# A routed-expert kernel on one core: rows gathered from three bf16 parts, an embedding normed later, a test moved forward

## The chip, the cores and the metric

The kernel runs on one core of a Trainium2 chip. The metric is device time in microseconds of one launch, as the median of several runs. TensorE (PE; its weight loads are PEld) multiplies, VectorE (DVE), ScalarE (ACT) and GpSimd (POOL) work on elements, and SyncE (SP) mostly issues transfers. POOL and ACT issue transfers too. Each engine works through its own queue in order, and engines wait for each other through semaphores.

## What is computed

Two transformer blocks, one behind the other, on 512 tokens of width 1024. The first ends in a layer of 64 experts in 8 groups: a token goes to its best group and the two best experts in it.

```
g_idx = top_k(softmax(h @ w_group + b_group), 1)
top_v, top_i = top_k(e_logits of that group, 2)
gate = g_w * softmax(top_v)
y[e] = (silu(x_e @ w1[e]) * (x_e @ w3[e])) @ w2[e]      # w1, w3: 1024 x 512, w2: 512 x 1024, fp32
out[token] += gate * y
```

The second block has retention and latent attention, a feed-forward layer, and at its end an embedding per layer (PLE):

```
e = rmsnorm(p @ w_ple_proj, ple_norm)
h = h + e * sigmoid(h @ w_ple_gate + b_ple_gate)
```

## The kernel before

All 64 experts are worked through in 16 groups of four (`q`), each expert with at most 32 tokens (`CAP`). The weights of the experts stream from memory in loads of 1 MB, in the order of `moe_specs`: for each group w1, w3, w2, each in two halves of four experts. SP issues them in that order from `moe_load_to`, as far ahead as slots are free. Each half product of `moe_up` or `moe_back` asks for loads 13 places ahead (`AHEAD`), and such a load waits until the product that used its slot is through.

Ahead of the experts stands the end of the attention. In the loop over four tiles of 128 tokens the last projection is added (`x_add`, L844), the rows are normed (L924, `x1n(t)`, fp32), transposed and scaled (`turn_tok`, `h` at L895) and multiplied to logits (L908). Then VectorE works out the routing in a chain of small operations (L953 to L978) that ends in `osel`, the selected experts in bf16. Products with a triangle of ones (L984 to L988) count for each token its place in its expert, and `places_oh(q)` compares places with 0 to 31 (L998), which gives the one-hot matrix `oh` of a group.

`moe_gather(q)` takes the rows of a group's tokens by multiplying: `x1n` is the stationary operand, `oh` the moving one, both fp32 (L1016), in two halves of 512 columns of the model. VectorE evacuates each half with the norm's gain (L1017) into `xT`. In group 0 the first half is gathered, then comes the first half product (L1029), then the second half of the gather, then the second half product. For the later groups the two halves of the gather of group q+1 stand between the half products of group q.

The PLE embedding is made at the same time, in units (`ple_units`) that a generator puts between other work: products and copies to `er` (L802), sums of squares (L823, L824), then the norm itself: ACT's scale (L806) and POOL's multiplication (L807) for tile 0, one VectorE operation each for the others (L814). POOL stores the normed tiles to memory (L808, L815). At the end of the kernel `ple_gate` loads them back and uses them (L1784 to L1789).

An expert with more than 32 tokens is left to `moe_rest`. It reads the largest count into a register on each engine (L1090) and branches (L1091); in this run the branch isn't taken. `REST_AT` = 8 puts it behind group 8, and `moe_lim` stops the loads at that point. On the way past the branch SP waits for the semaphores of its transfers.

Of the kernel before, what the change touches and what calls it, by code (L numbers as in the profile page):

```python
# [26 lines left out]
REST_AT = 8  # L27
# [44 lines left out]
def tile_kernel(ctx: ExitStack, tc: tile.TileContext, a: dict, dbg=None, upto=9):  # L72
# [712 lines left out]
    def ple_proj(pin, wst):  # L785
        pT = HL("pT", 2, 512, 2, M)
# [7 lines left out]
        lnb = bcast("lnb", a["ple_norm_2"])  # L794
        yield
        for t in range(NT):
            for nh in range(2):
# [7 lines left out]
                if t == 1 and nh == 1:  # L805
                    ACT.activation(ER[0], ER[0], AF.Copy, scale=ERS[0])  # L806
                    POOL.tensor_mul(ER[0], ER[0], lnb)  # L807
                    POOL.dma_start(e_d[0], ER[0])  # L808
# [4 lines left out]
        for t in (1, 2, 3):  # L813
            DVE.scalar_tensor_tensor(ER[t], ER[t], ERS[t], lnb, op0=ALU.mult, op1=ALU.mult)  # L814
            POOL.dma_start(e_d[t], ER[t])  # L815
            yield

    ERS = {}

    def ple_sums(t):  # L820

        rs = ERS[t] = sm("rs_e", (128, 1))
        POOL.tensor_scalar(rs, sum_sq(ER[t], D), 4.0 / D, 4.0 * EPS, op0=ALU.mult, op1=ALU.add)  # L823
        POOL.tensor_tensor(rs, rs, mhalf, op=ALU.pow)  # L824
# [29 lines left out]
    moe_w, moe_also, moe_n, moe_lim = {}, {}, [0], [24 * REST_AT + 37]  # L854

    def moe_load_to(n):
        n = min(n, moe_lim[0])
# [39 lines left out]

    h2 = {}
# [17 lines left out]
    for t in range(NT):  # L916
# [62 lines left out]
    ple_units(7)  # L979
# [15 lines left out]
    def places_oh(q):  # L995
        oh = Sx("oh", (128, NT, 4, 32))
# [11 lines left out]
    def moe_gather(q, hfs=range(2)):  # L1008
# [78 lines left out]
    def moe_rest():  # L1087
# [3 lines left out]
        with tc.If(most > CAP):  # L1091
            gov = Sx("gov", (128, NT, 64))
            DVE.scalar_tensor_tensor(gov, rk, CAP - NOT_SEL - 0.5, gate, op0=ALU.is_ge, op1=ALU.mult)
            hT_, hid, w2_, wk = L("hTo", (128, 8, 256)), M("hido", (128, 4, 256)), M("w2o"), [M("wko"), M("wko")]
            w2q = w2_.rearrange("p (j n) -> p j n", j=4)
            ps, s_, g1 = [PS() for _ in range(4)], Sx("so"), sm("g1", (128, NT))
            for ts in HALVES:
                for u, t in enumerate(ts):
                    for hf in range(2):
                        p = ps[2 * u + hf].rearrange("p (c s) -> p c s", c=4)  # L1100
                        for c in range(4):
                            PE.transpose(p[:, c], x1c(t)[:, 4 * hf + c], ident)
                        DVE.tensor_tensor(hT_[:, 4 * hf:4 * hf + 4, 128 * u:128 * u + 128], p,
                                          gr[:, 4 * hf:4 * hf + 4, None].to_broadcast([128, 4, 128]), op=ALU.mult)
# [733 lines left out]
```

## Time and profile before

| | us |
| --- | --- |
| median of 3 runs | 2050.45 |
| lowest and highest run | 2049.34, 2050.8 |
| profiled run | 2050.91 |
| span of the profiled run | 2048.8 |
| busy: PE, PEld | 1905.1, 1274.1 |
| busy: DVE, ACT, POOL | 744.6, 468.4, 208.8 |
| moved | 510.18 MB, 249 GB/s on the mean |

The page gives the busy time of each engine, then the span in 40 equal slices of 51.2 us with what the transfers moved in each. The share of an engine is a mean over stages with different limits: the attention ahead (up to about 337 us), the experts (to about 1320 us) and the second block behind. A timeline gives start, duration, engine, line, operation and names; in square brackets stands the idle time of the engine before it, and what ended that.

### The profile page before, as it was taken

To read this page: it belongs to the slowest core of one execution; us is meant where nothing else is said; L and a number is where in the kernel's file an instruction comes from. 1 tells how busy PE (TensorE), PEld (TensorE's weight loads), DVE (VectorE), ACT (ScalarE), POOL (GpSimd) and SP (SyncE) were. 2 spreads that over 40 slices of the span, in tenths; PEclk is the share of its full clock that TensorE was granted. 3 is DMA by queue.
4 is the path that set the end of the run, shared out by engine and by line. 5 is a ranking of instruction groups with operands and counts; after the bars stand their busy time and mean duration, and the time that the engine had idled before them with its cause. 6 is when DMAs were issued, how large, how long until landed. Compare 5 with 4: busy or idle time off the path is not lost.

```text
span 2048.8 us, 24118 instructions
## 1 busy us (share of the span) xinstructions
PE 1905.1 (93%) x9932; PEld 1274.1 (62%) x9932; DVE 744.6 (36%) x1392; ACT 468.4 (23%) x841; POOL 208.8 (10%) x159
## 2 busy tenths in 40 slices
PE   8999999998899888889988889799999999999998
PEld 6877778864344444434443434268877888888877
DVE  4364565421111111111112211157474642444465
ACT  5454433200000000000000100053235433323232
POOL 1010002200000000000000000044034310101031
PEclk9999999999999999999999999899999999999999
DMA  8122125799999999998999999973113214141342
GB/s 280 37 78 70 45 103 212 285 397 422 421 421 420 421 421 421 421 421 370 421 421 420 421 421 421 395 246 100 27 52 117 90 42 144 52 134 57 114 133 67
DMA packets 148725, 510.18 MB, mean 249 GB/s; under 512 B 20033, under 2 KB 77178, under 8 KB 100610
## 3 DMA queue, kind: packets, MB, share of 16 engines
q1 hardware_dynamic: 144226, 501.92, 62.8%
q0 software_dynamic: 1824, 6.31, 0.8%
q8 instruction: 80, 1.31, 0.3%
q10 hardware_dynamic: 2560, 0.35, 0.1%
q14 instruction: 35, 0.29, 0.0%
HBM read 502.24 MB, written 6.31 MB: 248 GB/s over the span
## 4 chain that ended last, share of the span: by engine, by line
PE 25%; DMA 18%; issue 5%; DVE 4%; ACT 1%; POOL 1%; SPq 0%; ACTq 0%; POOLq 0%; DVEq 0%
DMA w<-in_w_dram 18%; PE g L282 2%; PE g L284 2%; PE g L283 2%; PE u L282 1%; PE u L284 1%; PE u L283 1%; PE d L282 1%; PE d L284 1%; PE d L283 1%; PE pg L283 1%; PE pg L284 1%; PE pg L282 1%; PE ps L1029 1%; DVE h L1639 1%
## 5 line engine op out<-in xcount | busy, mean ns | idle before, releaser
L1029 PE MATMUL ps<-w,xT 128*32 128x512 f32 x2040 | 301.2, 627 | 60.2 <-DMA w<-in_w_dram 55.3
L1016 PEld LDWEIGHTS g<-oh,x1n 128*128 128x128 f32 x1024 | 246.2, 334 | 26.9 <-issue 19.3
L1016 PE MATMUL g<-oh,x1n 128*128 128x128 f32 x1024 | 252.3, 405 | 0.8 <-DVE oh L998 0.8
L1017 DVE TENSOR_TENSOR xT<-g,gr 128x512 f32<-128x512 f32 x32 | 22.1, 692 | 578.0 <-PE g L1016 578.0
L1029 PEld LDWEIGHTS ps<-w,xT 128*32 128x32 f32 x2040 | 71.4, 114 | 255.5 <-issue 128.6
L1043 PE MATMUL y<-w,hT 128*32 128x512 f32 x960 | 171.5, 686 | 48.3 <-DMA w<-in_w_dram 43.6
L1043 PEld LDWEIGHTS y<-w,hT 128*32 128x32 f32 x960 | 39.5, 122 | 166.6 <-DMA w<-in_w_dram 84.9
L1077 DVE TENSOR_TENSOR acc<-acc,spread 128x512 f32<-128x512 f32 x128 | 87.8, 688 | 122.7 <-PE spread L1072 122.7
L1072 PE MATMUL spread<-y,gt 128*128 128x512 f32 x256 | 118.4, 605 | 1.5 <-ACT y L1060 0.8
L226 POOL TENSOR_TENSOR c0l<-c0r,c0h 128x1024 fp32r<-128x1024 f32 x2 | 4.7, 2360 | 937.4 <-DMA c1r<-in_w_in_dram 937.4
L1280 ACT ACTIVATE hT<-hT 128x512 f32<-128x512 f32 x16 | 9.6, 597 | 360.8 <-PE hT L1278 360.8
L1072 PEld LDWEIGHTS spread<-y,gt 128*128 128x128 f32 x256 | 46.0, 189 | 73.3 <-issue 63.1
L1269 ACT ACTIVATE sl<-ps 128x512 f32<-128x512 f32 x16 | 9.6, 597 | 278.3 <-PE ps L1029 278.3
L1047 ACT COPY y<-y 128x512 f32<-128x512 f32 x30 | 17.6, 586 | 200.8 <-PE y L1043 194.9
L1704 POOL TENSOR_TENSOR aTl<-sg,aTh 128x512 fp32r<-128x512 f32 x18 | 23.4, 1297 | 225.9 <-ACT aTh L1703 178.5
L1702 DVE TENSOR_TENSOR sg<-sg,u 128x512 f32<-128x512 f32 x22 | 15.1, 688 | 72.0 <-PE u L284 70.9
L1703 ACT CAST aTh<-sg 128x512 fp32r<-128x512 f32 x22 | 13.7, 621 | 105.0 <-DVE sg L1702 105.0
L1271 DVE TENSOR_TENSOR hd<-sl,ps 128x512 f32<-128x512 f32 x16 | 11.0, 688 | 51.2 <-PE ps L1029 51.2
L174 POOL TENSOR_TENSOR rs<-ms,mhalf 128x1 f32<-128x1 f32 x20 | 12.0, 601 | 169.1 <-DVE ms L172 169.1
L1700 ACT ACTIVATE sg<-zg 128x512 f32<-128x512 f32 x22 | 13.9, 632 | 62.5 <-DVE zg L1699 62.5
L604 ACT ACTIVATE sc<-sc,mn 128x128 f32<-128x128 f32 (+3 forms) x32 | 17.7, 555 | 44.7 <-DVE mn L600 44.7
L768 POOL TENSOR_TENSOR mTl<-gl,mTh 128x512 fp32r<-128x512 f32 x8 | 11.5, 1454 | 157.7 <-PE ps L284 145.8
(1206 smaller groups left out, 3912.1 us busy)
## 6 DMA issues: line engine op xcount, KB each, us to landing
w<-in_w_dram SPq DMA_DIRECT2D x375, 1024.0 KB, 19.8
w<-in_w_dram SPq DMA_DIRECT2D x16, 512.0 KB, 13.9
x<-in_x_dram SPq DMA_DIRECT2D x4, 512.0 KB, 3.7
cb<-cum_d POOLq DMA_DIRECT2D x8, 256.0 KB, 3.6
acc<-in_x_dram SPq DMA_DIRECT2D x4, 512.0 KB, 7.5
e_d<-er POOLq DMA_DIRECT2D x4, 512.0 KB, 3.9
h_d<-u POOLq DMA_DIRECT2D x4, 512.0 KB, 6.6
h<-h_d SPq DMA_DIRECT2D x4, 512.0 KB
```

Of the source, the lines that this page charges most:

```text
L282: PE.matmul(out, ah, bh, start=(start and c == 0), stop=False)
L283: PE.matmul(out, ah, bl, start=False, stop=False)
L284: PE.matmul(out, al, bh, start=False, stop=(stop and c == kt - 1))
L604: ACT.activation(sc, sc, AF.Exp, bias=mn[:, s:s + 1], scale=-1.0, accum_out=su[:, s:s + 1])
L1016: PE.matmul(p[:, c], x1c(t)[:, 4 * hf + c], OHG[q][0][:, t].rearrange("p e s -> p (e s)"), start=(t == 0), stop=(t == NT - 1))
L1017: DVE.tensor_tensor(xT[:, 4 * hf:4 * hf + 4], p, gr[:, 4 * hf:4 * hf + 4, None].to_broadcast([128, 4, 128]), op=ALU.mult)
L1029: PE.matmul(p[32 * e:32 * e + 32], XT[q][:, 4 * hf + c, 32 * e:32 * e + 32], w[c] if isinstance(w, list) else w[:, c], start=(hf + c == 0) ...
L1043: PE.matmul(ps[nh][32 * e:32 * e + 32], HT[q][:, j, 32 * e:32 * e + 32], moe_w[2, q, hf, e][:, j - 2 * hf, 512 * nh:512 * nh + 512], start ...
L1072: PE.matmul(p, gt[:, t], Y[q][:, 512 * nh:512 * nh + 512], start=True, stop=True)
L1077: DVE.tensor_add(av(t)[:, sl], av(t)[:, sl], p)
L1639: DVE.tensor_add(av(t), av(t), v)
L1704: (eng or POOL).tensor_sub(aT.lo(c), s_, aT.hi(c).bitcast(F32))
```

## The change

- **Planes.** A new function `x_planes(t, eng)` splits each tile of `x1n` into three bf16 parts that add up to it: ACT casts the tile to `hi`, the engine `eng` subtracts it in place, ACT casts the rest to `mid`, the engine subtracts once more into `lo`. For tiles 0 and 1 the engine is VectorE, for 2 and 3 POOL. It is called in the loop over the tiles behind `logits_a(t - 1)`, for the last tile behind `logits_a(3)`.
- **Gather.** `oh` is bf16, and each fp32 product of the gather becomes three bf16 products into the same sum.
- **Group 0.** The whole gather stands ahead of the first product; the units of the embedding are all done before.
- **Test.** The largest count and its cast stand right behind the gather of group 0, and `moe_rest` behind the arithmetic of the gates, ahead of the first product. `REST_AT` and `moe_lim` go. The branch's body, not executed here, is rewritten for one tile at a time.
- **Embedding.** POOL stores the tiles without the norm, at the start of `ple_sums`. The scale is kept in `ers`, and `e_gain`, one VectorE operation for each of eight halves, applies scale and gain at the end. The gain `lnb`, 512 KB when it is spread over the partitions, is loaded at the end too.
- **Slots.** `pT` takes one slot of the weights' pool instead of two of the middle one.

```diff
+    def x_planes(t, eng):
+        hm = M("xb", (128, 2, 8, 128), BF)
+        if t % 2 == 0:
+            XL[t // 2] = M("xbl", (128, 2, 8, 128), BF)
+        v, XP[t] = x1c(t), (hm[:, 0], hm[:, 1], XL[t // 2][:, t % 2])
+        ACT.copy(XP[t][0], v)
+        eng.tensor_sub(v, v, XP[t][0])
+        ACT.copy(XP[t][1], v)
+        eng.tensor_sub(XP[t][2], v, XP[t][1])
...
             logits_a(t - 1)
+            x_planes(t - 1, POOL if t == 3 else DVE)
...
     logits_a(3)
+    x_planes(3, POOL)
...
-    ple_units(7)
+    ple_units(9)
...
-        oh = Sx("oh", (128, NT, 4, 32))
+        oh = Sx("oh", (128, NT, 4, 32), BF)
...
-                    PE.matmul(p[:, c], x1c(t)[:, 4 * hf + c], OHG[q][0][:, t].rearrange("p e s -> p (e s)"), start=(t == 0), stop=(t == NT - 1))
+                    for k in range(3):
+                        PE.matmul(p[:, c], XP[t][k][:, 4 * hf + c], OHG[q][0][:, t].rearrange("p e s -> p (e s)"),
+                                  start=(t == 0 and k == 0), stop=(t == NT - 1 and k == 2))
...
     places_oh(0)
-    ple_units(3)
-    moe_gather(0, (0,))
-    ple_units(1)
+    moe_gather(0)
     moe_load_to(15)
-    p1 = moe_up(0, 1, 0, lambda: moe_gather(0, (1,)))
...
+    cmax = const.tile([128, 1], F32, name="cmax")
+    DVE.tensor_reduce(cmax, pc[:, :64], axis=AX.X, op=ALU.max)
+    cmax_i = const.tile([128, 1], I32, name="cmax_i")
+    DVE.tensor_copy(cmax_i, cmax)
...
     DVE.tensor_tensor(gate, fl(oa), fl(ob), op=ALU.add)
+    moe_rest()
+    p1 = moe_up(0, 1, 0)
...
-        if q == REST_AT:
-            moe_rest()
-            moe_lim[0] = len(moe_specs)
...
-    bpl = bcast("bpl", a["b_ple_gate_2"])
+    bpl, lnb = bcast("bpl", a["b_ple_gate_2"]), bcast("lnb", a["ple_norm_2"])
...
+    def e_gain(k):
+        t, nh = divmod(k, 2)
+        DVE.scalar_tensor_tensor(es[k], es[k], ers[:, t:t + 1], lnb[:, 512 * nh:512 * nh + 512],
+                                 op0=ALU.mult, op1=ALU.mult)
...
+            if t == NT - 1 and nh == 1:
+                e_gain(2 * t + nh)
...
+            if n == 512:
+                e_gain(2 * t + nh)
```

What stands in a row on SP before, at the test behind group 8 (`w` are loads of weights, `cmax_i` is the largest count), and the way out of the branch:

```order
L880 DMA w_1104_5621<-in_w_dram 128x2048 [waits DMAHW7_49,PE_49]
L880 DMA w_1105_5623<-in_w_dram 128x2048 [waits DMAHW0_49,PE_49]
L1090 TENSOR_LOAD cmax_i [waits DVE_49]
L1090 ISA x2
...
L1091 UNCONDITIONAL_BRANCH [waits DMAHW0_49,DMAHW1_49,DMAHW2_49,DMAHW3_49,DMAHW4_49,DMAHW5_49,DMAHW6_49,DMAHW7_49]
```

There loads stand directly ahead of the test, and the branch waits for the semaphores of all eight. The same on SP after, in group 0 (`w13s` are the four pieces of the fifteenth weight):

```order
L867 DMA w13s_3550<-in_w_dram 128x512 [waits DMAHW3_49,DMASW4_49,Activation_49]
L867 DMA w13s_3551<-in_w_dram 128x512 [waits DMASW7_49,DMAHW4_49,DMASW0_49,DVE_49]
L867 DMA w13s_3552<-in_w_dram 128x512 [waits DMAHW5_49,Activation_49]
L1097 TENSOR_LOAD cmax_i [waits DVE_49]
L1097 ISA x2
L1098 COMPARE_AND_BRANCH
...
L1098 UNCONDITIONAL_BRANCH [waits DMAHW0_49,DMAHW1_49,DMAHW2_49,DMAHW3_49,DMAHW4_49,DMAHW5_49,DMAHW6_49,DMAHW7_49]
L870 DMA w_700_4213<-in_w_dram 128x2048 [waits DMAHW6_49,PE_49]
```

The test has moved behind the fifteen loads that fit the slots, and the sixteenth stands behind the branch. On VectorE before, in the loop over the tiles (`acc` are the rows, `wo` the projection's sum, `h` the scaled transposes, `lg` the logits):

```order
L895 TENSOR_TENSOR h_611_3153<-tt_3154,gr 128x512
L895 TENSOR_TENSOR h_611_3153<-tt_3160,gr 128x512
L908 TENSOR_TENSOR lg_2867<-lg_3166,rb 128x72
L844 TENSOR_TENSOR acc_2670<-acc_2670,wo_615_3176 128x512
L172 TENSOR_SCALAR ms_3204<-ss_3202 128x1
L924 TENSOR_SCALAR x1n_3208<-acc_2670,rs_3206 128x1024
```

and after, at the same place:

```order
L885 TENSOR_TENSOR h_611_3157<-tt_3158,gr 128x512
L885 TENSOR_TENSOR h_611_3157<-tt_3164,gr 128x512
L897 TENSOR_TENSOR x1n_3102<-x1n_3102,xb_3170 128x8x128
L899 TENSOR_TENSOR xbl_3118<-x1n_3102,xb_3170 128x1024
L911 TENSOR_TENSOR lg_2868<-lg_3175,rb 128x72
L835 TENSOR_TENSOR acc_2670<-acc_2670,wo_616_3185 128x512
L171 TENSOR_SCALAR ms_3213<-ss_3211 128x1
L927 TENSOR_SCALAR x1n_3217<-acc_2670,rs_3215 128x1024
```

The two subtractions of tile 1's planes now stand ahead of the addition of the projection of tile 3; those of tile 0 stand in the same way ahead of tile 2's.

## Rows read from the trace of the kernel before

**Rows 1.** The page's slices of the span: GB/s that the transfers moved in each.

```profile
GB/s 280 37 78 70 45 103 212 285 397 422 421 421 420 421 421 421 421 421 370 421 421 420 421 421 421 395 246 100 27 52 117 90 42 144 52 134 57 114 133 67
```

**Rows 2.** The page's groups (busy us, mean ns) and its transfers (count, KB, us to landing).

```profile
L1016 PE MATMUL g<-oh,x1n 128*128 128x128 f32 x1024 | 252.3, 405 | 0.8 <-DVE oh L998 0.8
...
w<-in_w_dram SPq DMA_DIRECT2D x375, 1024.0 KB, 19.8
```

**Rows 3.** Windows: length, busy PE, PEld, DVE, ACT, POOL, granted clock, DMA share, GB/s.

```profile
388.00:398.00 10.00, 8.45 (x40) 8.04 (x44) 5.60 (x9) 2.12 (x4) 5.61 (x9) 0.83 0.77 285
...
412.00:416.00 4.00, 4.00 (x44) 1.17 (x36) 3.13 (x15) 0.60 (x1) 0.00 (x0) 1.00 0.57 166
...
440.00:448.00 8.00, 8.00 (x74) 2.54 (x67) 0.00 (x0) 1.17 (x2) 0.00 (x0) 1.00 0.98 378
448.00:915.00 467.00, 414.23 (x2208) 206.10 (x2207) 78.25 (x160) 22.15 (x39) 0.00 (x0) 0.96 1.01 421
926.00:938.00 12.00, 12.00 (x65) 8.40 (x65) 1.24 (x2) 0.60 (x1) 0.00 (x0) 1.00 0.53 200
```

**Rows 4.** Timeline of SP's queue, 337 to 402 us: start, duration, what.

```profile
337.63 33.15 SPq L880 DMA_DIRECT2D w<-in_w_dram  x14
...
401.05 0.33 SPq L880 DMA_DIRECT2D w<-in_w_dram  x1
```

**Rows 5.** Timeline of SP's queue around the test behind group 8.

```profile
913.94 0.33 SPq L880 DMA_DIRECT2D w<-in_w_dram  x1
...
934.34 2.01 SPq L880 DMA_DIRECT2D w<-in_w_dram  x4
```

**Rows 6.** Timeline of TensorE at the test (PEq is its sequencer).

```profile
918.41 1.52 PE L1029 MATMUL ps<-w,xT 128*32 128x512 f32 x6 [3.35 <-PEq L1091]
```

**Rows 7.** Timeline of VectorE, 358 to 388 us.

```profile
358.16 1.28 DVE L895 TENSOR_TENSOR h<-tt,gr 128x512 f32<-128x512 f32 x2
361.07 0.69 DVE L844 TENSOR_TENSOR acc<-acc,wo 128x512 f32<-128x512 f32 x1 [1.62 <-PE wo L284]
...
369.21 0.69 DVE L844 TENSOR_TENSOR acc<-acc,wo 128x512 f32<-128x512 f32 x1 [3.28 <-PE wo L284]
...
379.08 0.23 DVE L908 TENSOR_TENSOR lg<-lg,rb 128x72 f32<-128x72 f32 x1 [2.94 <-PE lg L907]
...
384.31 0.42 DVE L975 TENSOR_TENSOR ob<-rt 128x256 f32<-128x256 f32 x1
384.75 2.52 DVE L978 TENSOR_TENSOR osel<-oa,ob 128x256 bf16<-128x256 f32 x1
```

**Rows 8.** Timeline of ACT: the sum of squares of a tile.

```profile
361.85 1.06 ACT L166 ACTIVATE junk<-acc 128x1024 bf16<-128x1024 f32 x1 [5.21 <-DVE acc L844]
```

**Rows 9.** Timeline of VectorE near the end: a split of a weight beside POOL.

```profile
2004.73 2.21 DVE L226 TENSOR_TENSOR pg12hl<-pg12r,pg12hl 128x1024 fp32r<-128x1024 f32 x1
```

**Rows 10.** Timeline of POOL beside the routing.

```profile
384.38 2.60 POOL L807 TENSOR_TENSOR er<-er,lnb 128x1024 f32<-128x1024 f32 x1 [1.26 <-ACT er L806]
```

**Rows 11.** Groups of POOL by form: busy us, mean ns.

```profile
L226 POOL TENSOR_TENSOR g00l<-g00r,g00h 128x1024 fp32r<-128x1024 f32 x2 | 6.7, 3367 | 0.4 <-POOL rs L174 0.2 <-ACT g00h L225 0.2
```

**Rows 12.** Timeline of TensorE, 386 to 390 us: bf16 products of 64 columns.

```profile
387.60 0.19 PE L985 MATMUL rk<-osel,trib 128*128 128x64 bf16 x1
387.63 0.28 PE L988 MATMUL ps<-osel,onesb 128*128 128x64 bf16 x4
```

**Rows 13.** Timeline of TensorE, 388 to 418 us: gather and first products.

```profile
388.72 7.88 PE L1016 MATMUL g<-oh,x1n 128*128 128x128 f32 x32 [0.81 <-DVE oh L998]
397.43 3.64 PE L1029 MATMUL ps<-w,xT 128*32 128x512 f32 x32 [0.83 <-issue]
401.00 7.89 PE L1016 MATMUL g<-oh,x1n 128*128 128x128 f32 x32
```

**Rows 14.** Timeline of VectorE at the end: the embedding's use, and a wait between halves.

```profile
2008.24 0.69 DVE L1788 SCALAR_TENSOR_TENSOR z__2308_12571<-z__2308_12571,e 128x512 f32<-128x512 f32 x1 [0.70 <-ACT z__2308_12571 L1785]
...
2043.39 0.76 DVE L1784 TENSOR_TENSOR z__2331_12814<-pg,bpl 128x256 f32<-128x256 f32 x2 [2.63 <-PE pg L284]
```

More of the change, by code (lines that the diff above doesn't have):

```diff
@@ L26 @@
 NOT_SEL = 1000.0
-REST_AT = 8
 TWO_PI = 6.283185307179586
@@ L793, in ple_proj @@
         wst.split(1)
-        lnb = bcast("lnb", a["ple_norm_2"])
         yield
@@ L804, in ple_proj @@
                     ple_sums(t - 1)
[L805 to L808, printed above, removed]
                 yield
@@ L812, in ple_proj @@
         yield
[L813 to L818, printed above, removed]
+    ers = const.tile([128, NT], F32, name="ers")
     def ple_sums(t):
-        rs = ERS[t] = sm("rs_e", (128, 1))
+        POOL.dma_start(e_d[t], ER[t])
+        rs = ers[:, t:t + 1]
         POOL.tensor_scalar(rs, sum_sq(ER[t], D), 4.0 / D, 4.0 * EPS, op0=ALU.mult, op1=ALU.add)
@@ L1093, in moe_rest @@
             DVE.scalar_tensor_tensor(gov, rk, CAP - NOT_SEL - 0.5, gate, op0=ALU.is_ge, op1=ALU.mult)
-            hT_, hid, w2_, wk = L("hTo", (128, 8, 256)), M("hido", (128, 4, 256)), M("w2o"), [M("wko"), M("wko")]
+            hT_, hid, w2_, wk = M("hTo", (128, 8, 128)), Sx("hido", (128, 4, 128)), M("w2o"), [M("wko"), M("wko")]
             w2q = w2_.rearrange("p (j n) -> p j n", j=4)
             ps, s_, g1 = [PS() for _ in range(4)], Sx("so"), sm("g1", (128, NT))
[L1097 to L1104, printed above, removed]
+            for t in range(NT):
+                for hf in range(2):
+                    p = ps[hf].rearrange("p (c s) -> p c s", c=4)
+                    for c in range(4):
+                        for k in range(3):
+                            PE.matmul(p[:, c], XP[t][k][:, 4 * hf + c], identb, start=(k == 0), stop=(k == 2))
+                    DVE.tensor_tensor(hT_[:, 4 * hf:4 * hf + 4], p,
+                                      gr[:, 4 * hf:4 * hf + 4, None].to_broadcast([128, 4, 128]), op=ALU.mult)
                 with tc.For_i(0, 64, 1) as i:
@@ L1112, in moe_rest @@
                                          [:, :, 128 * f:128 * f + 128])
-                            p = ps[2 * (f % 2) + k][:, 0:256]
+                            p = ps[2 * (f % 2) + k][:, 0:128]
                             for c in range(8):
                                 PE.matmul(p, w_[:, c], hT_[:, c], start=(c == 0), stop=(c == 7))
-                        pg, pu = ps[2 * (f % 2)][:, 0:256], ps[2 * (f % 2) + 1][:, 0:256]
-                        ACT.activation(s_[:, 0:256], pg, AF.Tanh, scale=0.5)
-                        DVE.scalar_tensor_tensor(s_[:, 0:256], s_[:, 0:256], 1.0, pg, op0=ALU.add, op1=ALU.mult)
-                        DVE.tensor_mul(hid[:, f], s_[:, 0:256], pu)
+                        pg, pu = ps[2 * (f % 2)][:, 0:128], ps[2 * (f % 2) + 1][:, 0:128]
+                        ACT.activation(s_[:, 0:128], pg, AF.Tanh, scale=0.5)
+                        DVE.scalar_tensor_tensor(s_[:, 0:128], s_[:, 0:128], 1.0, pg, op0=ALU.add, op1=ALU.mult)
+                        DVE.tensor_mul(hid[:, f], s_[:, 0:128], pu)
                     for n4 in range(4):
@@ L1122, in moe_rest @@
                         SP.dma_start(w2q, w2v[bass.ds(i, 1)].rearrange("o p j n -> (o p) j n")[:, :, sl])
[L1123 to L1129 removed]
+                        p = ps[n4 % 2][:, 0:256]
+                        for f in range(4):
+                            PE.matmul(p, hid[:, f], w2q[:, f], start=(f == 0), stop=(f == 3))
+                        DVE.scalar_tensor_tensor(av(t)[:, sl], p, g1[:, t:t + 1], av(t)[:, sl],
+                                                 op0=ALU.mult, op1=ALU.add)
     AHEAD = 13
     places_oh(0)
[L1133 to L1135 removed]
+    moe_gather(0)
     moe_load_to(15)
[L1137 removed]
+    cmax = const.tile([128, 1], F32, name="cmax")
+    DVE.tensor_reduce(cmax, pc[:, :64], axis=AX.X, op=ALU.max)
+    cmax_i = const.tile([128, 1], I32, name="cmax_i")
+    DVE.tensor_copy(cmax_i, cmax)
     gd = sm("gd", (128, NT, 8))
@@ L1158, in tile_kernel @@
     DVE.tensor_tensor(gate, fl(oa), fl(ob), op=ALU.add)
-    cmax = const.tile([128, 1], F32, name="cmax")
-    DVE.tensor_reduce(cmax, pc[:, :64], axis=AX.X, op=ALU.max)
-    cmax_i = const.tile([128, 1], I32, name="cmax_i")
-    DVE.tensor_copy(cmax_i, cmax)
+    moe_rest()
+    p1 = moe_up(0, 1, 0)
     dmp("rk", rk)
```

13 lines of the change are left out of this document (3 added, 10 removed).

## The prediction

> **What bounds the kernel now.** I read the page's forty slices first. From the ninth slice to the twenty-sixth the transfers run at 395 to 422 GB/s, and in the nineteenth alone they fall to 370 [rows 1]. There the experts' weights stream in, 375 loads of 1 MB and a few smaller ones; the gather of rows costs TensorE 252.3 us, but in the same stretch [rows 2]. Between 448 and 915 us the transfers stand at 421 GB/s without a hole, and TensorE is busy 414 of 467 us [rows 3]. So a microsecond in that stretch counts only if it is taken from the stream of loads: from its start, or from a hole in it. Before and after it (the attention, the second block) TensorE is the limit.
>
> The holes were read next. The first 14 loads leave SP from 337.63 us on; after them and one more weight in four pieces every slot is taken, and the next load goes out only at 401.05, when the first half product gives slots back [rows 4]. The transfers dip again at 412 to 416 (166 GB/s) and at 440 to 448 (378 GB/s) [rows 3]: the second half of the gather stands between the products, so slots come free late. The last hole, 926 to 938 at 200 GB/s, is the test: SP issues a load at 913.94 and nothing before 934.34 [rows 5]. In the not-taken branch SP waits until all its loads have landed, as its waits in the order show, and one takes 19.8 us from issue to landing [rows 2].
>
> **The test leaves group 8.** The hole is worth (421 - 200) / 421 x 12 us = 6.3 us [rows 3]: **-6.3**. The loads behind are all in the limiting stream, so I expect it back in full. TensorE's own price of the branch is 3.35 us [rows 6], which there hid behind the wait for loads.
>
> **The start of the stream.** Now the planes, the whole gather and the test stand ahead of the first product. I follow the chain to the first free slot.
>
> Planes of tiles 0 and 1, on DVE. Two subtractions of 128x1024, each at 1.28 us like the pair of 512-wide products [rows 7], with an ACT cast of 1.06 us between them, at the price of the square sum of the same shape [rows 8]. Tile 0's three steps, 3.6 us, follow h, which ended at 359.44; the addition behind them waited 1.62 us anyway and came at 361.07 [rows 7]. It now comes at 363.1: +2.0, which its tile's norm hands on. Tile 1's steps (h ends at 367.9 then, subtraction 369.2, cast 370.2, subtraction 371.5, a logits addition of 0.23) put the addition of 369.21 [rows 7] at 371.8: +2.6 in all. What follows keeps its pace, so the last logits, 379.08 [rows 7], are added at 381.7. Bounds: the planes read x1n with a stride, which no row of DVE shows. It can't gain; at the worst 0.93 us more for each of four subtractions (the DVE split of the pg weights beside POOL took 2.21 instead of 1.28 [rows 9]), +3.7. I take none: the nearest row without POOL beside it is h.
>
> Planes of tiles 2 and 3, on POOL. Each subtraction has the operands of the multiplication that took 2.60 us [rows 10]; ahead of it stands a cast. That gives about 375.4 to 378.0, 379.1 to 381.8, 381.8 to 384.4, 385.5 to 388.1. The routing chain, from the end of the last logits (379.31) to the end of osel (384.75 + 2.52 = 387.27), is 7.96 us [rows 7]. In it osel took 2.52 us where its neighbour of the same size took 0.42 [rows 7], while POOL multiplied a tile by the gain from 384.38 to 386.98 [rows 10]. Without these 2.1 us the chain is 5.86 us of work. Shifted by 2.6 it would start at 381.9, in the third subtraction, and meet the fourth. If every operation with two operands waits as osel did, the waits are 2.5 and 2.6 us, less about 0.9 for the reductions with one operand: osel ends at 381.9 + 5.9 + 4.2 = 392.0, **+4.7**. If one 2.1 us wait is all that is caught, as in the row, less what it overlaps, it ends at about 388.1, +0.8. I take 392.0: two long operations lie in the chain where there was one, and the one row there is shows a wait to POOL's end. At POOL's price beside DVE, 3.37 us [rows 11], the upper end is 4 x 0.77 = 3.1 us later.
>
> The Trainium skill ("SBUF — State Buffer", section "SBUF: two separate sides") speaks against this part: GpSimd and VectorE share a port pair as an exclusive lock, held for the whole instruction, against VectorE operations in a two-port mode or with two SBUF inputs. By that rule, the trace agrees: osel waited to the end of the multiplication. By the rule every such operation is held and osel ends at 392.0; by the one row read alone it ends at 388.1, which is the second case below.
>
> The gather. One bf16 product of 64 columns takes 0.19 us and four in a row 0.28, so each further one adds 0.03 us, its weight load included [rows 12]; 128 columns would add 0.06 at most, I take 0.057. 96 of them make 5.4 us, where a half of the fp32 gather took 7.88 [rows 13]. It starts 1.45 us after osel as now (388.72 - 387.27 [rows 7, 13]): 393.4 to 398.9. The evacuation and the step to the product cost 0.83 [rows 13], the maximum and its cast two small DVE operations of 0.23 [rows 7], the branch 3.35 [rows 6]: 403.5. The first half product, 3.64 [rows 13], frees slots at 407.1 instead of 401.05: **+6.1**. TensorE's clock was 0.83 on the mean from 388 to 398 [rows 3]; I charge the gather for it, 5.4 / 0.83 - 5.4 = **+1.1** (ends: 0, and 5.4 at half the clock). In exchange the two dips go, since products now follow each other: (421 - 166) / 421 x 4 = 2.4 and (421 - 378) / 421 x 8 = 0.8, **-3.2**. The start is worth 6.1 + 1.1 - 3.2 = **+4.0**.
>
> Behind the new wait stand, on SP, only loads for which no slot is free before 407; the 15 that are out have landed by then, so the drain costs nothing here. On DVE the arithmetic of the gates and group 1's one-hot matrices stand before or behind it, and TensorE asks for the second of them only after three half products, 403.5 + 3 x 3.6 = 414.3, over 10 us later.
>
> **At nothing.** The fp32 gathers of the fifteen later groups, hidden beside loads; if that cover were gone, they would give time back, not cost it. The embedding's norm: eight DVE operations of 0.69 us at the end. Seven stand where DVE waits 0.70 us for ACT's tanh, the last where it idles 2.63 us for TensorE [rows 14]. If that cover failed it would be 7 x 0.69 = 4.8 us. The removed multiplications and the ACT scale stood beside the gather; the gain vector's 512 KB move from a stretch without free slots to the end. The second block runs as before.
>
> **Sum.** The profiled run took 2050.91 us; -6.3 + 4.0 = -2.3 gives 2048.6. It lies 0.46 above the median of 2050.45, so the median forecast is 2048.1.
>
> **The rivals.** Faster: POOL hardly holds the routing. Then 3.9 us of the start are not lost, and -6.3 + 0.1 = -6.2 gives 2044.2; without the clock's 1.1 it is 2043.1. For it speaks that several routing operations run on 32 elements and may pass between POOL's; against it osel's 2.52 us.
>
> Slower: TensorE at the lower of its two clock levels (1.2 instead of 2.4 GHz) through the gather and the first half product, since nothing but short work precedes them. That is +5.4 on the gather instead of +1.1 and +3.6 on the product: the start is then worth 6.1 + 5.4 + 3.6 - 3.2 = 11.9, and -6.3 + 11.9 = +5.6 gives 2056.0. It decides from a start of more than 6.3 us. For it speaks the 0.83 of that stretch [rows 3]; against it, that the fp32 gather's two halves took 7.88 and 7.89 us, one in that stretch and one at the full clock [rows 13] and that the embedding's products fill the wait ahead.
>
> Not what it says: the stall only moves. If SP's drain holds the loads in group 0 as long as it did in group 8, because the four pieces of the fifteenth weight land late, the 6.3 us come back at the start, and the planes' 4.0 stay: 2050.45 + 4.0 = 2054.5. Against it stands that those pieces have over 10 us to land.
>
> **How the numbers follow.** The forecast 0.52, the faster rival 0.28, the slower 0.14, the moved stall 0.06. About 0.2% (4.1 us) is what a measurement of this kernel can tell from no change. Faster by more than that is under 2046.35: nearly all of the faster rival and a little of the forecast, 0.31. Slower, above 2054.55: most of the slower rival, and half of the moved stall, 0.15. In between 0.54. The forecast's own range is 2045 to 2054, from the hold and the strided reads. The range of 8 in 10 reaches to the faster rival and to the slower: 2043 to 2056.
>
> **What would show it.** In the profile after, SP's next load after the first fifteen at about 407 to 408, a stream at 421 GB/s from there to its end, no hole in the middle of it; the last logits near 381.7; routing operations of over 2 us beside POOL's subtractions; 96 products in 5.4 to 6.5 us; a gap of 3.35 us on TensorE behind them. It is wrong if the hole is found at another place, if the first free slot comes before 404 or after 412, or if DVE's wait for tanh at the end grows.

## The result, and the profile after

The changed kernel takes 2063.69 us (median of 4 runs, 2062.14 to 2063.7), the kernel before 2050.62 beside it: a ratio of 1.0061, interval 1.0048 to 1.0073. It is **slower by 13 us**, where 2048.1 was forecast with a range up to 2056. The profiled run took 2063.7, its span is 2061.9, 13.1 us over the 2048.8 of before.

Where the 13.1 us lie is read from five points that both traces have:

| point in the program | before | after | difference |
| --- | --- | --- | --- |
| SP's next load after the first fifteen | 401.05 | 418.62 | +17.6 |
| TensorE's last wait for up weights ends | 1315.86 | 1326.41 | +10.6 |
| the product behind it ends, `spread` begins | 1321.16 | 1332.94 | +11.8 |
| last addition of the feed-forward layer begins | 2000.29 | 2012.00 | +11.7 |
| end of the span | 2048.8 | 2061.9 | +13.1 |

The second and third points are these rows of TensorE's timeline, of before

```profile
1315.86 5.37 PE L1029 MATMUL ps<-w,xT 128*32 128x512 f32 x26 [0.66 <-DMA w<-in_w_dram]
1321.16 3.70 PE L1072 MATMUL spread<-y,gt 128*128 128x512 f32 x8
```

and of after:

```profile
1326.41 6.60 PE L1036 MATMUL ps<-w,xT 128*32 128x512 f32 x26 [1.49 <-DMA w<-in_w_dram]
1332.94 3.70 PE L1079 MATMUL spread<-y,gt 128*128 128x512 f32 x8
```

So 17.6 us are lost ahead of the first load, 7.0 are given back in the stream, and 2.6 are lost behind it, 1.2 in the last half product and 1.4 at the end. The page's slices (TensorE's clock in tenths of full speed, and GB/s; before in [rows 1]) show both the later start and what the change was to bring:

```profile
PEclk9999999889999999999999999999999999999999
...
GB/s 278 39 74 72 42 103 180 246 358 421 421 421 421 421 421 421 421 421 421 421 421 421 421 421 421 383 258 88 38 49 108 100 41 143 52 133 60 114 138 66
```

The nineteenth slice is at 421 now, where it was at 370: the hole in group 8 is gone. The ninth has fallen from 397 to 358. SP's queue shows the start, beside [rows 4]; the first row is the fourteenth load, `w13s` are the four pieces of the fifteenth weight:

```profile
399.44 0.33 SPq L870 DMA_DIRECT2D w<-in_w_dram  x1
399.86 2.79 SPq L867 DMA_DIRECT2D w13s<-in_w_dram  x4
418.62 0.35 SPq L870 DMA_DIRECT2D w<-in_w_dram  x1
```

The fourteenth load used to go out before 371 [rows 4]; now `pT` lies in a slot of the same pool, and the load leaves when the embedding's last product has ended (399.41). That costs nothing here: the transfers are down to 8 GB/s from 412 to 416, so both late loads have landed before a slot is free for the next one.

How 401 became 418 stands in VectorE's timeline (start, duration, line, names, in brackets the idle time before it), beside [rows 7]:

```profile
359.57 2.13 DVE L897 TENSOR_TENSOR x1n<-x1n,xb 128x1024 f32<-128x1024 f32 x1
363.81 2.18 DVE L899 TENSOR_TENSOR xbl<-x1n,xb 128x1024 bf16<-128x1024 f32 x1 [2.11 <-ACT xb L898]
365.92 0.66 DVE L835 TENSOR_TENSOR acc<-acc,wo 128x512 f32<-128x512 f32 x1
...
370.54 2.06 DVE L897 TENSOR_TENSOR x1n<-x1n,xb 128x1024 f32<-128x1024 f32 x1
374.81 1.99 DVE L899 TENSOR_TENSOR xbl<-x1n,xb 128x1024 bf16<-128x1024 f32 x1 [2.21 <-ACT xb L898]
...
376.86 0.68 DVE L835 TENSOR_TENSOR acc<-acc,wo 128x512 f32<-128x512 f32 x1
...
385.83 0.23 DVE L911 TENSOR_TENSOR lg<-lg,rb 128x72 f32<-128x72 f32 x1 [2.63 <-PE lg L910]
391.19 0.23 DVE L911 TENSOR_TENSOR lg<-lg,rb 128x72 f32<-128x72 f32 x1 [5.13 <-PE lg L910]
...
393.94 2.37 DVE L960 TENSOR_TENSOR ae<-rt,am 128x32 f32<-128x32 f32 x1
...
399.04 0.42 DVE L983 TENSOR_TENSOR osel<-oa,ob 128x256 bf16<-128x256 f32 x1
```

A subtraction of the planes takes 2.0 to 2.2 us, not 1.28, and DVE waits 2.1 to 2.2 us between two of them for ACT's cast, not 1.06. So the last addition of the projection comes at 376.86 (before 369.21, +7.65), and the last logits at 391.19 (before 379.08, +12.1): between the two another 4.5 us were lost. TensorE's rows and its clock say where:

```profile
380.53 1.94 PE L884 MATMUL tt<-cst,x1n 128*128 128x128 f32 x8 [6.70 <-DVE x1n L927]
382.26 3.52 PE L910 MATMUL lg<-wr,h 128*128 128x72 f32 x16
...
412.36 13.11 PE L1036 MATMUL ps<-w,xT 128*32 128x512 f32 x96 [5.93 <-SPq L1098]
```

```profile
376.00:380.00 4.00, 0.00 (x0) 0.00 (x0) 2.06 (x5) 2.37 (x3) 0.55 (x1) 0.59 1.01 426
380.00:384.00 4.00, 3.47 (x17) 3.50 (x18) 3.04 (x6) 1.18 (x2) 2.71 (x1) 0.50 1.02 428
384.00:388.00 4.00, 4.00 (x15) 3.52 (x15) 0.23 (x1) 4.00 (x3) 2.33 (x1) 0.50 0.79 322
...
408.00:412.00 4.00, 0.00 (x0) 0.00 (x0) 1.90 (x9) 0.21 (x1) 0.00 (x0) 0.85 0.53 202
412.00:416.00 4.00, 3.64 (x20) 1.13 (x24) 2.52 (x12) 0.00 (x0) 0.00 (x0) 0.50 0.03 8
```

(Windows of the changed kernel, columns as in [rows 3]; the granted clock is the sixth number after the length, leaving out the counts in brackets.) TensorE stood still for 6.70 us, waiting for tile 3's norm, its clock fell to 0.50, the lower of its two levels, and the last transposes and logits ran at it. The same happened again: 5.93 us of standing still at the test, and the first half product at 0.50, so that its slots came free 6.26 us after its start instead of 3.64 [rows 13]. The start in one sum: 12.1 until the logits, nothing in the routing (8.3 us to osel's end from the logits' start, before 8.2), -2.3 in the gather (5.6 us for the whole where a half took 7.88), 5.9 - 0.8 at the test, 2.6 in the product, 17.5 in all.

### The profile page after: what moved, and what is told of

It reads as the page before. It is cut to its first block, busy times and chain, and to the rows that moved or that the text cites. A ratio compares the mean times of both kernels' runs of the same rounds, so it can differ in the third digit from the quotient of the medians.

```text
span 2061.9 us, 25148 instructions
## 1 busy us (share of the span) xinstructions
PE 1824.7 (88%) x10444; PEld 1128.1 (55%) x10444; DVE 754.4 (37%) x1401; ACT 483.5 (23%) x848; POOL 215.4 (10%) x162
## 4 chain that ended last, share of the span: by engine, by line
DMA 43%; PE 25%; issue 5%; DVE 4%; ACT 1%; POOL 1%; SPq 0%; ACTq 0%; POOLq 0%; DVEq 0%
DMA w<-in_w_dram 43%; PE g L283 2%; PE g L281 2%; PE g L282 1%; PE u L281 1%; PE u L283 1%; PE u L282 1%; PE ps L1036 1%; PE d L283 1%; PE d L281 1%; PE d L282 1%; PE pg L282 1%; PE pg L283 1%; PE pg L281 1%; DVE h L1640 1%
## 5 line engine op out<-in xcount | busy, mean ns | idle before, releaser
L1036 PE MATMUL ps<-w,xT 128*32 128x512 f32 x2040 | 370.4, 642 | 124.2 <-DMA w<-in_w_dram 117.0
L1036 PEld LDWEIGHTS ps<-w,xT 128*32 128x32 f32 x2040 | 81.4, 116 | 375.7 <-DMA w<-in_w_dram 219.9
L1050 PE MATMUL y<-w,hT 128*32 128x512 f32 x960 | 178.3, 689 | 69.8 <-DMA w<-in_w_dram 65.4
L1022 PEld LDWEIGHTS <-xb 128*128 128x128 bf16 x1024 | 77.5, 98 | 26.4 <-issue 25.6
L1022 PE MATMUL g<-oh,xb 128*128 128x128 bf16 x1024 | 89.5, 219 | 0.7 <-DVE oh L1003 0.7
L1022 PE MATMUL g<-oh,xbl 128*128 128x128 bf16 x512 | 87.4, 219 | 0.0
L1054 ACT COPY y<-y 128x512 f32<-128x512 f32 x30 | 17.6, 585 | 229.1 <-PE y L1050 229.1
L1022 PEld LDWEIGHTS <-xbl 128*128 128x128 bf16 x512 | 50.1, 98 | 0.0
```

The source lines that it names most:

```text
L1022: PE.matmul(p[:, c], XP[t][k][:, 4 * hf + c], OHG[q][0][:, t].rearrange("p e s -> p (e s)"), start=(t == 0 and k == 0), stop=(t == NT - 1 ...
L1036: PE.matmul(p[32 * e:32 * e + 32], XT[q][:, 4 * hf + c, 32 * e:32 * e + 32], w[c] if isinstance(w, list) else w[:, c], start=(hf + c == 0) ...
L1050: PE.matmul(ps[nh][32 * e:32 * e + 32], HT[q][:, j, 32 * e:32 * e + 32], moe_w[2, q, hf, e][:, j - 2 * hf, 512 * nh:512 * nh + 512], start ...
L1054: ACT.copy(y[:, 512 * nh:512 * nh + 512], ps[nh])
```

## The experiments

Two theories for the 17.6 us at the start stood against each other: the planes (A), and the test in group 0 (B). Each ratio below is to the kernel before on the same chip.

**One: planes over the columns as they lie.**

```diff
...
-        v, XP[t] = x1c(t), (hm[:, 0], hm[:, 1], XL[t // 2][:, t % 2])
+        v, fp = x1n(t), (hm[:, 0], hm[:, 1], XL[t // 2][:, t % 2])
+        XP[t] = [f.rearrange("q (p c) -> q c p", c=8) for f in fp]
...
```

> The changed kernel with one thing different: the planes are made over the 1024 columns of a tile as they lie in memory, without the view that takes every eighth column, and the gather's weight loads read the bf16 planes with that step instead. Theory A (the strided reading is the cause: in the changed kernel DVE's plane subtractions took 2.13 us instead of the 1.28 of the sum, ACT's casts 2.1 instead of 1.06, the addition of the last projection came 7.65 us late, TensorE idled 6.7 us and then ran the logits at half its clock, 4.5 us more): subtractions of 1.28 us and casts of 1.06, the last logits near 382 instead of 391.2, the first load behind the test near 408 instead of 418.6, total near 2053. Theory B (the test in group 0 is the cause: a gap of 5.93 us on TensorE and the first half product at half the clock behind it, 2.6 us more): the planes are quicker, but the total stays within 3 us of 2063.7.

2052.75 us, ratio 1.0010 (1.0001 to 1.0020): 11 us of the 13 are gone. VectorE, in this run:

```profile
359.68 1.21 DVE L898 TENSOR_TENSOR x1n<-x1n,xb 128x1024 f32<-128x1024 f32 x1
362.01 1.23 DVE L900 TENSOR_TENSOR xbl<-x1n,xb 128x1024 bf16<-128x1024 f32 x1 [1.11 <-ACT xb L899]
...
371.40 0.68 DVE L835 TENSOR_TENSOR acc<-acc,wo 128x512 f32<-128x512 f32 x1
...
381.15 0.23 DVE L912 TENSOR_TENSOR lg<-lg,rb 128x72 f32<-128x72 f32 x1 [2.94 <-PE lg L911]
```

The step of eight columns cost 0.9 us on each DVE subtraction and 1.05 us on each ACT cast. On TensorE, which now reads the planes with that step, a weight load takes 147 ns instead of 98, and the gather 6.1 us instead of 5.6. The addition of tile 3 comes at 371.40 and the last logits at 381.15, as the prediction had them (371.8, 381.7). The next load is at 408.65. Theory A holds; but TensorE still stands 5.94 us at the test, so B isn't refuted.

**Two: the test back behind group 8.**

```diff
-    moe_rest()
     p1 = moe_up(0, 1, 0)
...
+        if q == REST_AT:
+            moe_rest()
+            moe_lim[0] = len(moe_specs)
```

> The changed kernel with the test put back behind group 8, with the limit on the loads there as in the kernel before (the branch's body, not executed, takes two weight slots for its tiles). Theory A (planes): the last logits stay at 391.2; the start gets better by the branch's own 3.35 us at the most, and the hole of 6.3 us comes back in group 8, so the total is 2063.7 - 3.4 + 6.3 = 2066.6 or more. Theory B (test): the gap of 5.93 us on TensorE shrinks to 0.8 and the first half product runs at the full clock, so the first slot is free near 411 instead of 418.6 (-7.7), and with the hole of 6.3 us the total is near 2062.3.

2056.33 us, ratio 1.0033 (1.0018 to 1.0047). With the strided planes the total is 7 us lower, more than either theory had. Of these, 4.5 us are won up to TensorE's last wait for weights; the rest lies behind it, with TensorE's clock (the last half product took 5.02 us at 0.72 of the full clock instead of 6.60 at 0.54, the last stretch 48.5 us instead of 49.9). On TensorE the first products follow the gather at once and at the full clock:

```profile
406.20 10.51 PE L1038 MATMUL ps<-w,xT 128*32 128x512 f32 x96
```

The next load goes out at 409.85 instead of 418.62, 8.8 us earlier (5.9 of the gap, the rest the product's clock), while TensorE's last wait for weights ends only 4.5 us earlier (1321.90 instead of 1326.41). So the hole in group 8, which is back, costs 4.3 us. Theory B holds as well; whether the two causes add up is asked in run five.

**Three and four: the hole alone.** First the kernel before without the test, then with the test but with the loads in the branch's body, which isn't executed, on POOL's queue.

```diff
-                            SP.dma_start(w_, wv[bass.ds(i, 1)].rearrange("o p c f -> (o p) c f")
+                            POOL.dma_start(w_, wv[bass.ds(i, 1)].rearrange("o p c f -> (o p) c f")
...
-                        SP.dma_start(w2q, w2v[bass.ds(i, 1)].rearrange("o p j n -> (o p) j n")[:, :, sl])
+                        POOL.dma_start(w2q, w2v[bass.ds(i, 1)].rearrange("o p j n -> (o p) j n")[:, :, sl])
```

> The kernel before without the test for overfull experts: the register load, the branch and its body are left out, and with them the limit on the loads. It measures the hole in group 8 alone. By bytes the hole is (421 - 200) / 421 x 12 = 6.3 us, so 2050.6 - 6.3 = 2044.3. The other reckoning is by the two traces: the changed kernel's stream was 14.4 us late by bytes at 450 us and TensorE's last waits for weights came 10.6 us late, so what the missing hole gave back was 3.8 us, which gives 2046.8 here.

> The kernel before with one thing different: in the branch's body, which is not executed, the loads are issued from POOL's queue instead of SP's. The way past the branch then has POOL wait for its own transfers, of which none is under way, and SP waits for nothing. If the hole is SP's wait for its loads to land, SP goes on issuing behind group 8, the hole is gone and the time is that of the kernel without the test, 2044 to 2047. If the hole is the price of a branch on all engines, it stays, and so does the time, 2050.6.

2046.88 us, ratio 0.9985 (0.9975 to 0.9994), and 2047.91, ratio 0.9986 (0.9976 to 0.9996). The second reckoning of the hole was right: TensorE's last wait ends at 1311.26 without the test, 4.6 us before the 1315.86 of before. In the fourth run it ends at 1313.32, but there the next load also went out 1.9 us later (402.90) than before. From that load to the last wait it is 914.8 us before and 910.4 in both runs, so the hole is worth 4.4 us. And the hole is SP's wait, not the branch, which the fourth run still has. SP's queue with the body on POOL:

```profile
902.13 30.84 SPq L880 DMA_DIRECT2D w<-in_w_dram  x13
935.13 3.76 SPq L866 DMA_DIRECT2D w<-in_w_dram  x2
```

Thirteen loads in a row, where SP stood from 914.27 to 934.34 [rows 5]. In group 8 the price of the branch not taken was set by which queue the untaken side uses.

**Five: all three findings put together.** Planes as they lie, test behind group 8, body's loads on POOL, all else as in the changed kernel.

> The changed kernel with three things different: planes made over the columns as they lie (first run), the test back behind group 8 with its limit on the loads (second run), and the branch's body, not executed, with its loads on POOL's queue (fourth run). If the three findings add up: first load after the first fifteen at 408.65 - 8.8 = 399.9 instead of the 401.05 of before, no dips behind it (2.5 us) and no hole in group 8 (4.5 us), so 1.2 + 2.5 + 4.5 = 8 us under before, 2042.5. The rival: with the start no later than before, the rest is set by TensorE's clock in the last group and at the end (1 to 3 us either way), and it is no better than the 2046.9 to 2047.9 of the kernels before without the hole.

2041.78 us, ratio 0.9951 (0.9934 to 0.9967): 10 us under the kernel before, 22 under the changed one. The next load goes out at 400.10, where 399.9 was reckoned, so the two causes add up:

```profile
400.10 0.33 SPq L872 DMA_DIRECT2D w<-in_w_dram  x1
400.52 6.77 SPq L858 DMA_DIRECT2D w<-in_w_dram  x8
```

**Six: TensorE kept busy.** To tell the clock from the planes, the embedding's first unit is done six times into the same sum, 6.8 us of products where TensorE had stood still; the planes stay strided.

```diff
-                mm3(p, pT, tk(t), wst.get(f"ple{nh}.0", look=False), ALL, 2)
+                for _ in range(6 if t + nh == 0 else 1):
+                    mm3(p, pT, tk(t), wst.get(f"ple{nh}.0", look=False), ALL, 2)
```

> The changed kernel with the first unit of the embedding's products done six times over into the same sum (the first five are overwritten), 6.8 us of products on TensorE ahead of the last tile's transposes, in the stretch from 373.8 to 380.5 where the changed kernel's TensorE idles. The planes stay as slow as they are. If the logits took 11.6 us instead of 7.1 behind the last norm because TensorE came out of an idle stretch at half its clock: full clock there, the last logits at 386.9 instead of 391.2, and the total 4 us less, 2059.5. If the logits wait for something else (ACT's casts in front of the embedding's copies, POOL), the last logits stay at 391 or come later, and the total stays at 2063.7.

The logits came as expected, the total did not: 2063.96 us, ratio 1.0062 (1.0045 to 1.0079). VectorE:

```profile
386.65 0.23 DVE L912 TENSOR_TENSOR lg<-lg,rb 128x72 f32<-128x72 f32 x1 [2.95 <-PE lg L911]
...
387.14 1.67 DVE L961 TENSOR_TENSOR ge<-lg,gm 128x32 f32<-128x32 f32 x1
...
391.11 2.81 DVE L962 TENSOR_TENSOR ae<-ae,cst 128x32 f32<-128x32 f32 x1
...
396.40 2.72 DVE L984 TENSOR_TENSOR osel<-oa,ob 128x256 bf16<-128x256 f32 x1
```

POOL, in the same run:

```profile
385.95 2.80 POOL L900 TENSOR_TENSOR xbl<-x1n,xb 128x1024 bf16<-128x1024 f32 x1 [2.28 <-ACT xb L899]
391.04 2.83 POOL L898 TENSOR_TENSOR x1n<-x1n,xb 128x1024 f32<-128x1024 f32 x1 [2.28 <-ACT xb L897]
396.05 2.79 POOL L900 TENSOR_TENSOR xbl<-x1n,xb 128x1024 bf16<-128x1024 f32 x1 [2.18 <-ACT xb L899]
```

At the full clock (1.00 from 376 to 388, where the changed kernel had 0.59 and 0.50) the last logits are at 386.65, 4.5 us earlier: TensorE's idle stretch was what slowed them. But now the routing falls beside three of POOL's subtractions instead of one, and each time one operation of 0.19 or 0.42 us lasts until POOL's ends (388.81 and 388.75; 393.92 and 393.87; 399.12 and 398.84). osel ends at 399.12, as in the changed kernel (399.46): up to there POOL's hold took what the clock gave back. In the changed kernel the logits were simply late enough to miss two of the three. Then run six loses more: TensorE has run out of embedding products and stands for 4.3 us before osel, its clock is 0.57 from 400 to 404, the gather takes 7.0 us instead of 5.6 and the first slots come 7.8 us after the first product's start, so the next load goes out at 421.10, 2.5 us later than in the changed kernel. The totals agree only because of what lies behind the stream: in the profiled runs 1.6 us come back in the last half product (5.03 instead of 6.60) and 1.4 in the last stretch.

**Seven: the embedding's part alone,** in the kernel before (raw tiles stored, `e_gain` at the end, `lnb` loaded there).

> The kernel before with the embedding's part of the change alone: raw tiles stored, scale and gain applied at the end, the gain loaded there. In the changed kernel the stretch from the second half of the gate's products to the end was 1.5 us longer than before, where TensorE waited 2.72 us instead of 1.41 for the split of a weight and ran at 0.66 behind it. If that comes from the embedding at the end (DVE's queue, or 512 KB more ahead of the weights): +1.5, 2052.1. If it is only where TensorE's clock fell in that run, and the eight operations hide: 2050.6 within 0.5, DVE's wait for tanh gone and nothing else moved. That the embedding's multiplications are gone beside the routing could give 2.1 us back at osel; then it is 2048.5.

2051.2 us beside 2052.1, ratio 0.9996 (0.9987 to 1.0006): no difference. From the last addition of the feed-forward layer to the end it is 48.4 to 48.8 us in the profiles of before and of the third run, and in five with the late embedding (second, fifth, sixth, tenth and twelfth). It is 49.8 to 50.0 in six others with the late embedding, the changed kernel among them, and 51.3 in the fourth, with the early one. So the late embedding by itself doesn't cost the 1.4 us at the end of the changed kernel. The third alternative fails too: osel ends at 384.98, 2.3 us earlier than before, but the products behind it wait until TensorE is through with the embedding's products, and VectorE's next step comes only 0.4 us earlier (387.83 before):

```profile
387.45 0.42 DVE L982 SCALAR_TENSOR_TENSOR rk<-osel,rk 128x256 f32<-128x256 bf16 x1 [2.46 <-PE rk L977]
```

So in the kernel before, POOL's hold on osel cost next to nothing.

**Eight: no planes, the gather in fp32** and whole ahead of the first product; test and embedding as in the changed kernel.

```diff
-                    for k in range(3):
-                        PE.matmul(p[:, c], XP[t][k][:, 4 * hf + c], ...)
+                    PE.matmul(p[:, c], x1c(t)[:, 4 * hf + c], ...)
```

> The changed kernel without the planes and with fp32 one-hot matrices: the gather is the fp32 one of before, but whole ahead of the first product, and test and embedding stand as in the changed kernel. It tells what the bf16 planes cost in all. Reckoned from rows: last logits at 379.1 as before, osel at 385.2 to 387.3, gather of 15.8 us to about 403.5, a gap of 5.9 us for the test, 409.4, the first half product 3.6 to 6.2 us, first load at 413 to 415.6; then 12 to 14.6 later than before, less 2.5 for the dips and 4.5 for the hole: +5 to +7.6, total 2055.6 to 2058.2, that is 6 to 8 us under the changed kernel. If the planes were what made the start late by themselves, it would be at 2051 or lower.

2060.94 us beside 2052.1, ratio 1.0047 (1.0031 to 1.0064): +8.8 us where +5 to +7.6 was reckoned. The profiled run shows 1.1 of the rest in the last half product (6.49 instead of 5.37) and 1.4 at the end. Its next load is at 414.94, within the 413 to 415.6. Whole gather and test ahead of the first product make most of the loss even without planes: by the ratios (1.0061, 1.0047, 1.0010) the strided planes add about 3 us to it, and planes in order take between 7 and 8 away.

**Nine and ten: who makes the planes.** The fifth kernel with all subtractions on POOL, and with all on DVE.

> The fifth run's kernel with one thing different: the plane subtractions of tiles 0 and 1 are on POOL, as those of 2 and 3, so none is on DVE. If DVE's subtractions ahead of the additions of the projection are what is left of the planes on the path (the addition of tile 3 at 371.3 instead of 369.1): addition at 369.2, last logits near 379.0 instead of 381.05, first load near 398 instead of 400.1, total 2 us less, 2039.8. If POOL's port hold shifts the same time to DVE (norm and products of tile 1 and 2 wait for POOL's 2.1 to 2.7 us): no change or worse, 2041.8 and more.

> The fifth run's kernel with all plane subtractions on DVE, so that POOL holds nothing. The routing's two longer operations (0.72 and 1.23 us instead of 0.19) go back to 0.19, -1.6 us; in exchange four subtractions of 1.22 us stand on DVE between the norm of tile 3 and the routing, of which two fit into its waits. If the hold is the smaller price: osel ends at 388.7 + 4.9 - 1.6 - 1.2 = 390.8, total 2 us more, 2043.9. If the hold was the larger price: osel ends before 388.7 and the total is under 2041.8.

All on POOL: 2041.97 us, ratio 0.9954 (0.9938 to 0.9971), the same as the fifth. The next load comes 1.1 us earlier, at 399.00, not 2: POOL's subtraction for tile 1 (364.84 to 366.99) now holds the norm of tile 2, one operation that takes 0.75 us elsewhere:

```profile
364.91 2.63 DVE L930 TENSOR_SCALAR x1n<-acc,rs 128x1024 f32<-128x1024 f32 x1 [0.90 <-POOL rs L174]
```

All on DVE: 2044.96 us, ratio 0.9973 (0.9963 to 0.9983), next load at 401.18, osel's end at 390.08 instead of 388.74. By these points the hold is the smaller price, as the first alternative had it; the intervals of the ratios overlap with those of the fifth and the ninth run, so the totals alone don't show it.

**Eleven: is the gap at the test SP's drain?** The changed kernel with the body's loads on POOL.

> The changed kernel with one thing different: the loads in the branch's body, not executed, are on POOL's queue, so SP waits for nothing on the way past the branch. In the changed kernel TensorE stood 5.93 us between the gather and the first product, and SP's drain stood in group 0. If the gap is the branch itself, on every engine (0.83 + 0.4 + 3.35 us and 1.3 more): the gap stays near 5.9, the first load stays near 418.6, total 2063.7. If the drain of the fifteenth weight's four pieces holds it: the gap falls to 4.6 or less and the total by 1.3 us and by what the first half product gains at a higher clock, up to 4 us.

2063.08 us, ratio 1.0054 (1.0037 to 1.0071), next load at 419.37. TensorE:

```profile
413.60 11.61 PE L1036 MATMUL ps<-w,xT 128*32 128x512 f32 x84 [5.96 <-PEq L1098]
```

The gap is the same without a drain, so in group 0 it is the branch on the engines, and the rival of the moved stall falls. It was closer than the prediction thought: the fourteenth and fifteenth loads left at 399.4 to 402.7, not at 371 and 385 as before, and in the changed kernel the row of the first product names SP as the one that came last. In the four other kernels with the test in group 0 it is TensorE's own sequencer.

**Twelve: halves as before,** in the ninth kernel: half the gather, the first half product, the other half.

```diff
-    moe_gather(0)
+    moe_gather(0, (0,))
     moe_load_to(15)
+    p1 = moe_up(0, 1, 0, lambda: moe_gather(0, (1,)))
...
-    p1 = moe_up(0, 1, 0)
```

> The ninth run's kernel with group 0 as in the kernel before: half of the gather, the first half product, the other half of the gather, the second half product. A bf16 half takes 2.8 us, so the first slots are free 2.8 us earlier, near 395.3 if the ninth run's are at 398. Four loads take 10 us to move, and the next slots come 3.6 + 0.8 + 2.8 us after the first, so no dip comes back: total 2.8 us less than the ninth run's. If the order of loads or TensorE's clock takes it back: no change against the ninth run.

The next load goes out at 396.20, 2.8 us earlier, with no dip behind it, and TensorE's last wait ends 2.1 us earlier (1305.44 against 1307.51). The medians don't show it: 2041.06 us, ratio 0.9957 (0.994 to 0.9973). Between the last wait and the end lie 2 to 4 us that go with TensorE's clock: the last half product took 3.6 us in some profiles and 5.0 to 6.6 in others. The fifth, ninth and twelfth kernels beat both kernels of this case, by 9 to 10 us against before, and can't be told apart.

## Why the prediction was wrong

The mechanisms named were mostly there; two sizes on the path were wrong, and one effect was put at the wrong place. One of the prediction's own signs of being wrong showed: the first free slot came at 418.6, where it was to come before 412.

- **Planes on DVE and ACT: the step that failed.** It priced subtraction and cast by rows that read columns in order (1.28 and 1.06) and said that no row shows the strided read. Its upper bound of 3.7 us covered DVE alone; ACT's casts, two on the path, had no bound at all, and they doubled too. Measured: +7.65 at the addition of tile 3 where +2.6 was taken, so even with the bound of 3.7 the step falls short (6.3). With columns in order the step's own numbers hold within 0.6 us (run one). The Trainium skill ("SBUF — State Buffer", section "Door 1: The DMA port swizzle (why `[64,N]` ≈ `[32,N]`)") has a note on lines of 16 bytes: reads that go to a new line each time pay, so fp32 may step by up to four. Here the step is eight, and the trace agrees: 2.13 instead of 1.21 us on DVE, 2.05 instead of 1.05 on ACT. The note gives no price, but it speaks against the value taken, that of columns in order.
- **What an idle TensorE costs.** The sum had the clock only as 1.1 us on the gather. The gather ran at the full clock (5.6 us, 5.4 forecast); the clock fell at two other places, at the logits (4.5 us, run six) and at the first half product (2.6). The slower rival had the right mechanism and the right product, though not the gather, and it gave as cause that only short work precedes them. What preceded the lower clock here was TensorE standing still, for 6.7 and 5.9 us, and for 4.3 in run six.
- **POOL's hold on the routing.** Right as a mechanism: every long operation of the chain ended with a subtraction of POOL's. Its size was not: 4.2 us of waits were taken. In the changed kernel the chain took 8.0 us with one operation held, as before. It came out at nothing only because the chain started, at 391.4, behind the third subtraction (to 391.02), one of the two that it was to meet; with run six's earlier start it met three. In run one it met the two of the forecast and lost 1.6 us, since there POOL's subtractions took 2.1 us and each operation came in the midst of one.
- **The test's own gap.** Forecast 0.83 + 0.46 + 3.35 = 4.6 from the gather's end to the first product, measured 5.4 to 6.0 in five kernels. And 0.83 belonged to a product that waits for its half; behind a whole gather the first half product waits for nothing (run two), so all of the gap is the test's. Nor was 3.35 the branch's price [rows 6]: in all eight kernels with the test in group 8 the first product behind it starts 7.0 to 7.2 us after the last wait for weights of the half product ahead, and the gap is what is left of that: 3.35 to 3.6 behind 3.6 us of products, 1.06 to 1.40 behind 5.6 to 6.0 (clock 0.63 in run four, 0.60 in run nine). The price was known to be on the path, but it wasn't asked whether it had to be there.
- **The hole.** 6.3 us by bytes, 4.1 to 4.4 from the next load to TensorE's last wait: 914.8 us before and in run seven, 910.4 without the hole (runs three and four), 912.1 without the dips (run two), 907.5 to 908.5 without either, in eight kernels, and 909.2 in run twelve. So the dips, forecast at 3.2, were worth 2.5 to 2.8.
- **Right:** the 15 later gathers and the embedding at no price (run seven), the drain in group 0 at no price (run eleven), though by a small margin, SP's drain as the cause of the hole (run four), the gather's 96 products.

Run one shows how much of the start is luck where it comes right. With columns in order the next load goes out at 408.65, and 408.2 was forecast. But osel ends there 3.2 us before the 392.0 of the forecast, and the test's gap (5.9 instead of 4.6) and the first half product at the lower clock (6.1 instead of 3.6) give that time away again.

So: 17.6 at the start instead of 7.2 (5.1 more by the planes, 4.5 and 2.6 by the clock, 1.3 at the test, less 2.0 for the hold and 1.1 for the gather), -7.0 in the stream instead of -9.5, and 2.6 us by the clock at the end of the experts and of the kernel, which stood in no step.

Open is why the hole gives TensorE back some 2 us less than its bytes, and what the branch does in its time: in group 0 the first product starts 4.3 to 4.9 us behind the count in the five kernels (412.36 - 407.47 = 4.9 in the changed one). Open is also what sets the clock in the last half product and in the last stretch.

## What to carry to other kernels

Price an elementwise step by a row with the same access pattern, not only the same shape, and put a bound on every engine of its chain; a view that costs a gather's weight loads little (0.5 us over 96 products) can double the time of a subtraction and a cast, so let the engine with room take the step. A wait on TensorE's path of the length seen here (5.9 and 6.7 us) cost twice: once itself, and again in what ran at the lower clock behind it. Taking a hold away helps only where nothing else holds the next step: in run seven osel came 2.3 us earlier, the step behind it 0.4. Before a rarely taken branch is moved to save its stall, look at what the stall waits for: here it was a queue used on the side that isn't taken, and moving that use to another queue took the stall away where it stood.

## What had not been expected of the hardware

- The step of eight fp32 columns (32 bytes) doubled ACT's cast, 2.03 to 2.26 us against 1.03 to 1.05, and took DVE's subtraction from 1.21 to 2.13; on POOL it was 2.7 to 2.9 against 2.1 to 2.6. A bf16 weight load of 128 columns with a step of 16 bytes went from 98 to 147 ns, most of it beside the products.
- POOL's subtraction also held a DVE operation with one tile operand and a scalar for each row: 2.63 us instead of 0.75 (run nine).
- The length of the last half product (3.62 to 6.60 us) and of the last stretch (48.4 to 51.3 us) changed between kernels that are the same there, with TensorE's clock: 3.62 us at 1.00 in run one, 5.37 at 0.67 before, 6.60 at 0.54 in the changed kernel. A difference of 2 us in one profile says nothing about a change in this kernel.
